# Both output projections of a two-layer encoder by 2x2 blocks with seven block products

## The chip, the core and the metric

The kernel runs on one core of a Trainium2 chip. The metric is the device time of one execution in microseconds. A core has TensorE (PE) for matmuls and transposes, VectorE (DVE), ScalarE (ACT) and GpSimd (POOL) for elementwise work, and SyncE (SP), which here only issues DMAs. Each engine runs its own list of instructions in order; they wait for each other by semaphores.

## What is computed

Two layers over 1024 tokens of width 1024, all in float32. Layer 0 mixes tokens by window attention (16 heads of 64), layer 1 by a gated recurrence in both directions (8 heads of 128); both add four cross-attention heads of 128 into 256 memory tokens. The mixer's output has 1024 + 512 = 1536 columns and goes through one output projection `w_out` (1536 x 1024). Cut to what matters here:

```python
o = jnp.concatenate([o, memory_cross_attn(xq, mem_kv)], axis=-1)   # 1024 x 1536
y = o @ w_out                                                     # the output projection
h = h + rmsnorm(y, norm_g[layer, 1])
v = rmsnorm(h, norm_g[layer, 2])
gate, up = jnp.split(v @ w_in, 2, axis=-1)
f = (jax.nn.gelu(dwconv_centred(gate, conv_w, conv_b)) * up) @ w_out_ffn
h = h + rmsnorm(f, norm_g[layer, 3])
```

## The kernel before

Every float32 product is made of three matmuls: each operand x is split into a high part (a cast by ScalarE) and the rest (a subtraction by VectorE), and hi·hi, lo·hi and hi·lo are summed in PSUM (`mm3`, lines 84 to 86 of the profile; `mmk`, line 529, in the FFN; `split`, lines 89 and 90; `wunit`, lines 79 and 80, for a weight of 128x1024). Inputs come through four stage buffers `st`.

The attention of layer 0 (`window`) goes by four groups of heads: `proj(g)` projects, `attend(g)` does eight blocks of scores, softmax and products with v (tiles `ps`, `pt`, `po`), and the four cross heads are put in as units by the table `XU`. Layer 1 (`hgrn`) goes by eight heads. Both write their outputs, transposed, to DRAM: `oT[l]` has twelve blocks of 128 rows by 1024 tokens, eight of the mixer, four of the cross heads; two blocks are a pair.

The output projection is the class `WOut`. It loads `oT` by token tile (`or`), splits it (`oh`, `ol`), and for each of 8 token tiles, 2 column halves and 12 row blocks issues three matmuls of 128x512 into a PSUM tile `pb`. Its weights are 12 units per layer (`wh`, `xwh`); the first column half stays in `y0` until the second is done. Behind each token tile of the second half come the tile's steps: sum of squares, scale by the norm, add to the residual `x`, store to `h1d`, and `norm_T`, which norms it for the FFN (`nu`, line 115), transposes it by TensorE (`pt`, line 119) and splits it into `uh` and `ul`. Part of the projection begins early: `open` and `early` issue its matmuls among the last attention group and the last head, for the blocks that are there already. A scheduler in the tile framework merges these lists into each engine's order at build time.

The FFN (`ffn`) has both its products by 2x2 blocks with seven block products in place of eight. Its second product has a list `SECOND` of (product, pair) units, `unit` loads a weight block and a block of hidden tokens into one `st` buffer of 128x1024 and splits it, `mms` issues 12 matmuls with it (four token tiles, tiles `X` and `V`). Sums of weight blocks are made in DRAM by accumulating DMAs of GpSimd's queue (`second_sums`), one step at each `sum_steps[l].send(...)`; sums of hidden blocks are made by VectorE and stored in `hid`. The steps behind it, per token tile, are `tail` (lines 790 to 794) and `norm_T`; the first token half's tails come behind pairs 1, 3, 5 and 7 of product 5, the second half's in product 3, for which the last units are held.

## Time and profile before

| | |
|---|---|
| median of 3 runs | 2732.68 us (2732.43 to 2733.03) |
| profiled execution | 2730.88 us, span 2729.1 us |
| mean granted TensorE clock | 0.993 |
| PE busy | 2659.9 us, 97% of the span |
| DVE, ACT, POOL busy | 1825.5, 1390.7, 468.9 us |
| layer 0's projection | about 433.7 (first matmul, among attention) to 597.1 us |
| layer 1's projection | ends at about 2091.5 us |

Times are microseconds from the span's start. In rows of the timeline stand start, duration, engine, line, operation, output<-inputs, form, count, and in brackets the engine's idle time just before and the instruction that ended it. The matmuls overlap in the pipeline, so that the duration of one (0.39 us for 128x512) is longer than the step from one to the next.

### The profile page before, as it was taken

The numbers are of one execution on the slowest core, as the hardware profiler recorded it, in microseconds if no ns is written. First come the engines' busy times: TensorE is split into PE (matmuls) and PEld (weight loads), VectorE is DVE, ScalarE is ACT, GpSimd is POOL, SyncE is SP. The second block draws the span as 40 slices with busy tenths as digits, with TensorE's granted clock in tenths as the row PEclk, the third lists the DMA queues.
The fourth block names the chain that finished last, engine by engine and source line by source line (L and its number), as shares of the span: only waits on it lengthen the run. The fifth ranks groups of instructions, "written<-read, shape, count | busy, mean of one in ns | idle before, by whom it ended". The sixth has DMA issues, their size and how long they took to land.

```text
span 2729.1 us, 37480 instructions
## 1 busy us (share of the span) xinstructions
PE 2659.9 (97%) x13496; PEld 2231.1 (82%) x13496; DVE 1825.5 (67%) x3031; ACT 1390.7 (51%) x2550; POOL 468.9 (17%) x517
## 2 busy tenths in 40 slices
PE   8999998999999999999999999999899999999998
PEld 7888897788888888877888888888788788888886
DVE  6587777578565565477686777868566856566446
ACT  6367666544444444454444545545454444444443
POOL 1231120111111100032232231312121111110013
PEclk9999998999999999999999999999999999999999
DMA  7673213656777757674234541111466587775656
GB/s 278 212 167 95 59 45 100 193 193 150 204 201 194 204 151 241 195 246 140 81 129 114 118 90 55 43 58 34 133 216 171 156 207 202 203 198 158 225 194 228
DMA packets 213580, 428.45 MB, mean 157 GB/s; under 512 B 20369, under 2 KB 77073, under 8 KB 207761
## 3 DMA queue, kind: packets, MB, share of 16 engines
q1 hardware_dynamic: 187264, 333.50, 37.6%
q0 software_dynamic: 23680, 88.09, 15.6%
q10 hardware_dynamic: 2448, 4.46, 0.5%
q8 instruction: 106, 1.74, 0.3%
q14 instruction: 82, 0.66, 0.1%
HBM read 333.17 MB, written 117.96 MB: 165 GB/s over the span
## 4 chain that ended last, share of the span: by engine, by line
PE 86%; DVE 8%; DMA 2%; ACT 2%; issue 2%; POOL 1%; SPq 0%; DVEq 0%; POOLq 0%; ACTq 0%
PE X L529 26%; PE V L529 11%; PE pj L84 7%; PE pj L85 7%; PE pj L86 7%; PE Y L529 5%; PE pb L85 3%; PE pb L84 3%; PE pb L86 3%; PE po L1110 1%; PE pt L341 1%; PE pa L1062 1%; PE pa L1042 1%; PE pu L1086 1%; PE pt L119 1%
## 5 line engine op out<-in xcount | busy, mean ns | idle before, releaser
L90 DVE TENSOR_TENSOR wl<-st,wh 128x1024 fp32r<-128x1024 f32 (+1 forms) x234 | 258.7, 1110 | 338.5 <-ACT wh L89 332.6
L89 ACT CAST wh<-st 128x1024 fp32r<-128x1024 f32 (+1 forms) x234 | 219.1, 938 | 288.1 <-PE X L529 180.2
L84 PE MATMUL pj<-uh,wh 128*128 128x512 f32 x512 | 205.8, 402 | 6.4 <-DVE xl L90 4.6
L529 PE MATMUL X<-wl,wh 128*128 128x512 f32 x528 | 205.1, 390 | 0.1
L529 PE MATMUL X<-wh,wl 128*128 128x512 f32 x528 | 205.0, 390 | 0.0
L86 PE MATMUL pj<-uh,wl 128*128 128x512 f32 x512 | 202.8, 396 | 0.0
L529 PE MATMUL X<-wh 128*128 128x512 f32 x528 | 200.3, 390 | 2.4 <-DVE c L838 1.7
L85 PE MATMUL pj<-ul,wh 128*128 128x512 f32 x512 | 202.2, 395 | 0.1
L84 PE MATMUL pj<-wh,uh 128*128 128x384 f32 (+1 forms) x512 | 191.0, 373 | 0.4 <-DVE v L283 0.4
L85 PE MATMUL pj<-wl,uh 128*128 128x384 f32 (+1 forms) x512 | 187.0, 365 | 0.0
L86 PE MATMUL pj<-wh,ul 128*128 128x384 f32 (+1 forms) x512 | 186.8, 365 | 0.0
L529 PE MATMUL V<-uh,wh 128*128 128x512 f32 x344 | 133.9, 389 | 0.3 <-ACT uh L89 0.3
L529 PE MATMUL V<-ul,wh 128*128 128x512 f32 x344 | 133.9, 389 | 0.0
L529 PE MATMUL V<-uh,wl 128*128 128x512 f32 x344 | 133.9, 389 | 0.0
L80 DVE TENSOR_TENSOR wl<-st,wh 128x1024 fp32r<-128x1024 f32 (+1 forms) x93 | 115.7, 1252 | 25.0 <-ACT wh L79 24.1
L79 ACT CAST wh<-st 128x1024 fp32r<-128x1024 f32 (+1 forms) x103 | 103.9, 1016 | 46.1 <-PE pj L85 27.2
L529 PEld LDWEIGHTS X<-wh 128*128 128x128 f32 x528 | 99.1, 188 | 24.3 <-issue 2.6
L84 PEld LDWEIGHTS pj<-uh,wh 128*128 128x128 f32 x512 | 97.0, 189 | 26.5 <-DVE xl L90 5.5
L1056 POOL TENSOR_TENSOR E<-EP,q 128x256 f32<-128x256 f32 x64 | 54.5, 851 | 371.6 <-DVE EP L1049 292.9
L529 PEld LDWEIGHTS X<-wl,wh 128*128 128x128 f32 x528 | 99.1, 188 | 21.1 <-DVE wl L90 0.5
L529 PEld LDWEIGHTS X<-wh,wl 128*128 128x128 f32 x528 | 99.1, 188 | 20.6
L86 PEld LDWEIGHTS pj<-uh,wl 128*128 128x128 f32 x512 | 96.6, 189 | 19.4
(337 smaller groups left out, 7332.7 us busy)
## 6 DMA issues: line engine op xcount, KB each, us to landing
st<-hid SPq DMA_DIRECT2D x154, 256.0 KB, 3.0
st<-in_ffw_dram SPq DMA_DIRECT2D x106, 256.0 KB, 3.0
w2s<-in_ffw_dram POOLq DMA_DIRECT2D x24, 1024.0 KB, 8.0
st<-in_ffw_dram SPq DMA_DIRECT2D x48, 512.0 KB, 3.6
hid<-tt SPq DMA_DIRECT2D x88, 256.0 KB, 4.5
st<-w2s SPq DMA_DIRECT2D x88, 256.0 KB, 3.1
sx<-in_ffw_dram SPq DMA_DIRECT2D x80, 256.0 KB, 3.9
sy<-in_ffw_dram SPq DMA_DIRECT2D x40, 512.0 KB, 5.7
```

What stands on the lines that cost most here:

```text
L79: act.copy(h[:, :n], raw)
L80: (eng or dve).tensor_tensor(l[:, :n], raw, h[:, :n].bitcast(F32), op=ALU.subtract)
L84: pe.matmul(o, ah, bh, start=first, stop=False)
L85: pe.matmul(o, ah, bl, start=False, stop=False)
L86: pe.matmul(o, al, bh, start=False, stop=last)
L89: act.copy(h, src)
L90: dve.tensor_tensor(l, src, h.bitcast(F32), op=ALU.subtract)
L119: pe.transpose(ps[:, k, :], u[:, (4 * b + k) * P:(4 * b + k + 1) * P], ident)
L341: pe.transpose(tp[:, j, :], sm[:, j, c * P:(c + 1) * P], ident)
L529: pe.matmul(o, x, y, start=new, stop=e, skip_group_check=not first)
L1042: pe.matmul(pa[:, c, :], E2[:, cs], E1[:, cs], start=True, stop=True)
L1056: pool.tensor_tensor(gl, pl_, ql, op=ALU.mult)
```

## The change

The projection is taken out of `WOut` and put on the code of the FFN's second product, which becomes a class `Second` that both use. With the token blocks (rows of the output) split in two halves of 512 tokens, the row blocks in even and odd ones, and the columns of `w_out` in two halves of 512, seven block products replace eight. Per layer there are 7 products x 6 pairs = 42 units, each a weight block and a token block of 128x512, with 12 matmuls a unit, four token tiles of three. The order of products is 1, 2, 6, 7, 4, 5, 3 and that of pairs 0, 1, 2, 4, 5, 3.

`token_sums` makes the sums of token blocks for a pair: it loads two blocks of `oT` into two of the four `st` buffers, does four VectorE operations of 512 columns and stores the buffers to `os`. Sums of weight blocks (`wos`) come from `weight_sums`, 12 more steps ahead of the FFN's 18. The tails come behind pairs 1 to 4 of product 5 and, for the second half, in product 3. `early` issues product 1 of four pairs for three token tiles (layer 0) or two (layer 1) among the last attention group and the last head. Two cross units move from the third attention group to the fourth (`XU`). The first FFN weight is no longer loaded ahead in its own pool.

```diff
-WOUT_POOL = ((0, 1, 2), ())
-XU = [(0, 2), (0, 2), (2, 2), (0, 0)]
+XU = [(0, 2), (0, 2), (2, 0), (2, 0)]
+OLAST, OHOLD = 6, 4
+OPAIRS = (0, 1, 2, 4, 5, 3)
...
-    def second_sums(l):
+    def weight_sums(l):
...
+        for w, o, rs in ((A[f"wout{l}"], wosum[l], (slice(0, 3), slice(3, 6))),
+                         (A["ffw2"][l], w2sum[l], (slice(0, 4), slice(4, 8), slice(8, NP2)))):
+            steps += [(o, r, a, f, n, x, y) for a, f, n, x, y in ((0, 0, 1, w, None), (1, 0, 1, w, None), (2, 2, 2, w, None),
+                                                                  (0, 1, 2, w, True), (2, 0, 1, o, True), (3, 2, 1, o, True)) for r in rs]
...
+    def token_sums(l, p, halves):
+        i, j = (slice(b * 512, (b + 1) * 512) for b in halves)
+        e, c = [stg.tile([P, 1024], F32, tag="st", name="st") for _ in range(2)]
+        nc.sync.dma_start(e, oT[l][2 * p])
+        nc.sync.dma_start(c, oT[l][2 * p + 1])
+        dve.tensor_tensor(c[:, j], c[:, j], e[:, j], op=ALU.subtract)
+        dve.tensor_tensor(e[:, j], e[:, i], e[:, j], op=ALU.subtract)
+        dve.tensor_tensor(e[:, i], c[:, j], e[:, i], op=ALU.add)
+        dve.tensor_tensor(c[:, i], e[:, i], c[:, i], op=ALU.subtract)
+        nc.sync.dma_start(osum[l][p, 0], e)
+        nc.sync.dma_start(osum[l][p, 1], c)
...
         for g in range(3):
             attend(g, cur)
             cur = proj(g + 1)
+            token_sums(0, g, (0, 1))
+            if g == 2:
+                token_sums(0, 4, (0, 1))
+        attend(3, cur)
+        bank = lambda pl, tag, n: pl.tile([P, 512], F32, tag=tag, bufs=n, name=tag)
+        X = lambda t: bank(*((psq, "pj", 2), (psq, "pj", 2), (psq, "ptq", 1), (psp, "po", 1))[t])
+        V = lambda t: bank(psp, *(("ps", 2), ("pt", 2))[t // 2])
+        wo0.early(X, (0, 1, 2), 4)
+        token_sums(0, 5, (0, 1))
+        token_sums(0, 3, (0, 1))
         ea.release()
         ap_.release()
+        wo0.open()
+        return X, V, tags["pt"], (psp, psq)
...
+    class Second:
...
+        def unit(self, k, p):
+            r = stg.tile([P, 2, 512], F32, tag="st", name="st")
+            for i, x in enumerate(self.source(k, p)):
+                nc.sync.dma_start(r[:, i, :], x)
+            held = k == 3 and 0 <= self.pairs.index(p) - (len(self.pairs) - self.last) < self.hold
+            h, l_ = [(self.hold_pool if held else ring).tile([P, 1024], F32R, tag=t, name=t) for t in ("wh", "wl")]
+            r = r.rearrange("p a b -> p (a b)")
+            if k == 6:
+                nsplit(h[:, :512], l_[:, :512], r[:, :512])
+                split(h[:, 512:], l_[:, 512:], r[:, 512:])
+            else:
+                split(h, l_, r)
+            return h, l_
+        def ahead(self):
+            if self.todo and len(self.made) < (self.last if self.todo[0][0] == 3 else 3):
+                self.made.append(self.unit(*self.todo.pop(0)))
+        def mms(self, u, ps, ts_, first):
+            h, l_ = u
+            for t in ts_:
+                m = slice(512 + t * P, 512 + (t + 1) * P)
+                mmk(ps[t], 1, lambda _: (h[:, m], l_[:, m]), lambda _: (h[:, :512], l_[:, :512]), first)
+        def early(self, X, ts_, n):
+            self.X = {t: X(t) for t in ts_}
+            for i in range(n):
+                self.begun.append(self.unit(*self.todo.pop(0)))
+                self.mms(self.begun[-1], self.X, ts_, i == 0)
...
+        def run(self, X, V, free, gy, gx, src, dst, halves):
...
+            tails = (1, 3, 5, 7) if n > 8 else (1, 2, 3, 4)
...
+            for k in self.order:
+                if k == 5:
+                    self.X = {t: X(t) for t in (2, 3, 0, 1)}
+                elif k == 2:
+                    self.V = {t: V(t) for t in range(4)}
+                ps = self.V if k == 2 else self.X
+                hold = []
+                for i, p in enumerate(self.pairs):
+                    if k == 1 and self.begun:
+                        u = self.begun.pop(0)
+                        self.mms(u, ps, rest, i == 0)
+                        self.ahead()
+                        continue
+                    while len(self.made) < 1:
+                        self.ahead()
+                    u = self.made.pop(0)
+                    self.ahead()
+                    if k == 3 and i >= n - self.last:
+                        hold.append(u)
+                    else:
+                        self.mms(u, ps, range(4), k in (1, 5, 2) and i == 0)
+                    if k == 5 and i in tails:
+                        t = tails.index(i)
+                        tail(ia, t, y["c11"][:, t, :], ss["q11"][:, t:t + 1], y["c21"][:, t, :], ss["q21"][:, t:t + 1])
+                for t in range(4):
+                    if k in (1, 6, 7, 4):
+                        act.copy(y[{1: "c11", 6: "c12", 7: "c22", 4: "c21"}[k]][:, t, :], ps[t])
+                    elif k in (2, 5):
+                        q = y[{2: "c11", 5: "c22"}[k]][:, t, :]
+                        dve.tensor_tensor(q, ps[t], q, op=ALU.add)
+                    else:
+                        for u in hold:
+                            self.mms(u, ps, (t,), False)
+                        sb = np_.tile([P, 1], F32, tag="sb", name="sb")
+                        y1 = np_.tile([P, 512], F32, tag="y1", name="y1")
+                        dve.tensor_tensor(y1, ps[t], y["c12"][:, t, :], op=ALU.add)
+                        sumsq(np_, y1, sb)
+                        dve.tensor_tensor(y1, y1, g3[:, D0], op=ALU.mult)
+                        tail(ib, t, y1, sb, y["c22"][:, t, :], ss["q22"][:, t:t + 1])
+                if k == 4:
+                    scaled("c21", "q21", D1)
+                elif k == 5:
+                    scaled("c22", "q22", D1)
+                elif k == 2:
+                    scaled("c11", "q11", D0)
+                    pst[0] = free()
...
+    where = {1: (2, None), 2: (3, None), 4: (1, None), 5: (None, 0), 7: (None, 1), 6: (None, 2), 3: (None, 3)}
+    def block_of(k, p, w, s):
+        a_, d_ = where[k]
+        return w[p, a_] if d_ is None else s[p][d_]
+    def out_proj(l, halves):
+        i, j = (slice(b * 512, (b + 1) * 512) for b in halves)
+        def source(k, p):
+            raw = {1: (0, i), 2: (1, i), 3: (1, j)}
+            made = {6: (0, i), 5: (0, j), 4: (1, i), 7: (1, j)}
+            t = oT[l][2 * p + raw[k][0]][:, raw[k][1]] if k in raw else osum[l][p, made[k][0]][:, made[k][1]]
+            return block_of(k, p, A[f"wout{l}"], wosum[l]), t
+        return Second(l, "wo", OPAIRS, (1, 2, 6, 7, 4, 5, 3), source, OLAST, OHOLD)
...
-                    wo1.early(psj, 2, es)
+                    wo1.early(XB, (0, 1), 4)
             if h == 7:
+                token_sums(1, 5, (1, 0))
...
-                wo1.open(2, 0)
+                wo1.open()
...
+                for p in {1: (0,), 3: (1,), 5: (2, 4)}.get(h, ()):
+                    token_sums(1, p, (1, 0))
+        token_sums(1, 3, (1, 0))
...
-    window()
-    wo0.finish()
-    ffn(0, wo0, h2d, True, (0, 1), (0, 1))
-    hgrn()
-    wo1.finish()
-    ffn(1, wo1, out, False, (1, 0), (1, 0))
+    finish_out(0, wo0, window(), A["x"], (0, 1))
+    ffn(0, h2d, True, (0, 1), (0, 1))
+    finish_out(1, wo1, hgrn(), h2d, (1, 0))```

TensorE's order at the end of layer 0's projection, before (`pb` is the projection, `pt` the transposes of a tile, `X` and `Y` the FFN's first products; the last transposes come 49 rows later):

```order
L85 MATMUL pb_6450<-xwl_5791,oh_6493 128x512
L86 MATMUL pb_6450<-xwh_5790,ol_6494 128x512
L119 MATMUL pt_6436<-ident_74,nu_6429 128x128 x4
L119 MATMUL pt_6443<-ident_74,nu_6429 128x128 x4
L529 MATMUL X_6576<-uh_78,xwh_5796 128x512
L529 MATMUL X_6576<-ul_79,xwh_5796 128x512
...
L529 MATMUL Y_6577<-uh_78,wl_6571 128x512
L529 MATMUL X_6741<-uh_78,wh_6729 128x512
L119 MATMUL pt_6528<-ident_74,nu_6521 128x128 x4
L119 MATMUL pt_6535<-ident_74,nu_6521 128x128 x4
L529 MATMUL X_6741<-ul_79,wh_6729 128x512
```

And now, at the same place (`po` is the last token tile of product 3):

```order
L414 MATMUL po_5978<-wl_6261,wh_6260 128x512
L414 MATMUL po_5978<-wh_6260,wl_6261 128x512
L121 MATMUL pt_6194<-ident_74,nu_6187 128x128 x4
L121 MATMUL pt_6201<-ident_74,nu_6187 128x128 x4
L121 MATMUL pt_6307<-ident_74,nu_6300 128x128 x4
L121 MATMUL pt_6314<-ident_74,nu_6300 128x128 x4
L121 MATMUL pt_6364<-ident_74,nu_6357 128x128 x4
L121 MATMUL pt_6371<-ident_74,nu_6357 128x128 x4
L121 MATMUL pt_6421<-ident_74,nu_6414 128x128 x4
L121 MATMUL pt_6428<-ident_74,nu_6414 128x128 x4
L121 MATMUL pt_6478<-ident_74,nu_6471 128x128 x4
L121 MATMUL pt_6485<-ident_74,nu_6471 128x128 x4
L414 MATMUL X_6531<-uh_78,wh_6519 128x512
```

Five tiles' transposes stand between the projection and the FFN, where two tiles' did, one of them inside the FFN's products. Layer 1 has the same.

SyncE's order where layer 0's projection begins, before (`o` are the attention's last outputs, `or` loads for the projection):

```order
L352 DMA oT0_57<-o_5087 64x2x256 x2
L447 DMA or_5623<-oT0_57 128x2x128
L447 DMA or_5639<-oT0_57 128x6x128
L107 DMA g1_5752<-in_norm_g_dram 128x1024
L107 DMA g2_5754<-in_norm_g_dram 128x1024
```

And now (`st_5356` and `st_5357` are the last token sums, `st_5393` and `st_5403` the last two units of product 1, `st_5413` the first of product 2, in the buffer of `st_5356`):

```order
L370 DMA oT0_57<-o_5145 64x2x256 x2
L154 DMA st_5356<-oT0_57 128x1024
L155 DMA st_5357<-oT0_57 128x1024
L109 DMA g3_5384<-in_norm_g_dram 128x1024
L109 DMA g0_5386<-in_norm_g_dram 128x1024
L435 DMA st_5393<-in_wout0_dram 128x512
L435 DMA st_5393<-oT0_57 128x512
L435 DMA st_5403<-in_wout0_dram 128x512
...
L160 DMA os0_84<-st_5356 128x1024
L161 DMA os0_84<-st_5357 128x1024
L435 DMA st_5413<-in_wout0_dram 128x512
```

A load, four operations and a store stand now between the last output and the loads of product 2.

TensorE's order at the last head of layer 1, before (`po` is the head's output product, `pt` its transposes, 18 rows of `pb` stand between):

```order
L1110 MATMUL po_18099<-S_17366,qin_17364 128x128
L84 MATMUL pb_17859<-xwh_18025,oh_18037 128x512
L85 MATMUL pb_17859<-xwl_18026,oh_18037 128x512
...
L1120 MATMUL pt_18129<-ident_74,on_18124 128x128 x4
L84 MATMUL pb_17902<-xwh_18031,oh_18169 128x512
```

And now (`X` and `pa` are product 1 of the projection):

```order
L1057 MATMUL po_18034<-S_17374,qin_17372 128x128
L1067 MATMUL pt_18064<-ident_74,on_18059 128x128 x4
L414 MATMUL X_17845<-wh_18106 128x512
L414 MATMUL X_17846<-wh_18106 128x512
L414 MATMUL pa_18095<-wh_18106 128x512
```

The head's transposes follow its product at once, and the rest of product 1 follows them.

338 lines of the change are left out of this document (84 added, 254 removed).

## The prediction

> **What bounds the kernel now.** I read the page first. Its rows of busy time and its chain of waits say that TensorE is the kernel:
>
> ```profile
> span 2729.1 us, 37480 instructions
> PE 2659.9 (97%) x13496; PEld 2231.1 (82%) x13496; DVE 1825.5 (67%) x3031; ACT 1390.7 (51%) x2550; POOL 468.9 (17%) x517
> PE 86%; DVE 8%; DMA 2%; ACT 2%; issue 2%; POOL 1%; SPq 0%; DVEq 0%; POOLq 0%; ACTq 0%
> ```
>
> Only 69.2 us of the span are without a matmul. So removed matmuls are worth their full time, but only where TensorE has something else to run meanwhile. The windows show the price of one matmul and the places where TensorE starves already (columns: stretch, length, then busy time and instructions of PE, PEld, DVE, ACT and POOL, granted clock, DMA share, GB/s):
>
> ```profile
> 780.00:840.00 60.00, 60.00 (x266) 49.70 (x265) 33.27 (x36) 26.41 (x34) 8.21 (x10) 1.00 0.79 199
> 400.00:420.00 20.00, 14.27 (x67) 10.80 (x66) 15.86 (x46) 13.43 (x34) 10.66 (x9) 0.87 0.45 145
> 420.00:440.00 20.00, 16.34 (x73) 12.47 (x73) 16.16 (x36) 14.36 (x30) 0.00 (x0) 0.79 0.37 116
> 480.00:500.00 20.00, 17.76 (x89) 13.93 (x88) 11.72 (x21) 12.29 (x27) 0.00 (x0) 1.00 0.25 66
> ```
>
> The first row is the code of the FFN's second product: 60.00/266 gives 0.2256 us per 128x512 matmul; I use 0.2265 (the timeline's rows step by 0.22 to 0.23). The other rows are layer 0's last attention group; after its last projection matmul at 405 us it runs with nothing beside it until the old out-projection begins to fill it:
>
> ```profile
> 405.17 0.38 PE L289 MATMUL ptq<-ident,rq 128*128 128x128 f32 x2
> 433.70 0.50 PE L84 MATMUL pb<-wh,oh 128*128 128x512 f32 x1 [0.68 <-ACT oh L89]
> ```
>
> From 405 to 434 us TensorE idles 5.7 + 3.7 = 9.4 us and its clock falls to 0.8; from 480 to 500 it idles 2.2.
>
> **What it removes.** Per layer the projection has 8 tiles x 2 halves x 12 blocks x 3 = 576 matmuls; seven products of 6 pairs x 4 tiles x 3 are 504. Both layers: 144 x 0.2265 = **-32.6 us**, all on the path. The added splits (42 units of 1024 columns against about 36) and the token sums (24 operations of 0.6 us per layer) lie in stretches like 780 to 840, where VectorE is busy 33 of 60 us; I cost them at nothing there. If that cover went, 12 splits and 24 sums would be 28 us a layer. The weight sums are queued on GpSimd, busy 17%, and paced by steps of the projections and the recurrence far ahead: nothing.
>
> **What it adds at the end of each projection.** Before, the tail of a token tile (add, norm, transposes) comes every 8 us under the next tile's 36 matmuls, and the FFN begins before the last tile is done:
>
> ```profile
> 596.25 1.06 PE L119 MATMUL pt<-ident,nu 128*128 128x128 f32 x8 [0.91 <-DVE nu L115]
> 597.07 0.48 PE L529 MATMUL X<-uh,xwh 128*128 128x512 f32 x1
> 608.47 1.04 PE L119 MATMUL pt<-ident,nu 128*128 128x128 f32 x8
> ```
>
> It costs 0.9 us: the last transposes at 608.47 come inside the FFN's products. Now all eight tails fall into the last two products, and TensorE's order has 40 transposes, each behind VectorE, between the last product and the first FFN matmul. That matmul needs only the first eight of them (the last tile of the first token half) but stands behind all. VectorE's spacing is in these rows:
>
> ```profile
> 1207.38 1.29 DVE L115 SCALAR_TENSOR_TENSOR nu<-x,nrs,g 128x1024 f32<-128x1024 f32 x1 [0.73 <-POOL nrs L96]
> 1208.59 1.22 DVE L90 TENSOR_TENSOR wl<-st,wh 128x1024 fp32r<-128x1024 f32 x1
> 1209.72 0.68 DVE L838 TENSOR_TENSOR c<-X,c 128x512 f32<-128x512 f32 x1
> 1210.32 1.22 DVE L90 TENSOR_TENSOR wl<-st,wh 128x1024 fp32r<-128x1024 f32 x1
> ...
> 1231.75 0.68 DVE L844 TENSOR_TENSOR y<-X,c 128x512 f32<-128x512 f32 x1
> ...
> 1234.84 0.75 DVE L794 SCALAR_TENSOR_TENSOR x<-y,prs,x 128x512 f32<-128x512 f32 x1 [0.66 <-POOL prs L96]
> 1235.51 0.74 DVE L794 SCALAR_TENSOR_TENSOR x<-c,prs,x 128x512 f32<-128x512 f32 x1
> ```
>
> From start to start: a split 1.13, an operation of 512 columns 0.60, a scaled add 0.66, the norm multiply 1.2. From the start of product 5 VectorE has 13 splits (14.7), 16 scaled adds (10.6), 8 norm multiplies (9.6), 16 transposed splits (9.6), 12 adds and multiplies (7.2) and 24 small ones of about 0.1 (2.4): 54 us, and some 4 us of chain waits like the 0.73 and 0.66 above, 58 in all. TensorE has in the same time 12 pairs x 12 x 0.2265 = 32.6 and 64 transposes (8 in 1.04), 8.3: 41 us. It waits 17.3 us. The same tail code already stands behind FFN 0, where the next layer's projections cover it:
>
> ```profile
> 1241.92 0.39 PE L529 MATMUL X<-wh,wl 128*128 128x512 f32 x1
> ...
> 1263.55 0.66 PE L119 MATMUL pt<-ident,nu 128*128 128x128 f32 x4 [0.28 <-DVE ul L90]
> ```
>
> From the last product to the last transposes are 21.9 us, of which the 32 transposes take 4: 18 without cover. Two ways give 17 to 18; I take 17.3. After such a wait the clock is low for a while, as it was here:
>
> ```profile
> 79.00 0.33 PE L289 MATMUL ptq<-ident,rq 128*128 128x128 f32 x1 [2.02 <-POOL rq L279]
> ...
> 80.40 0.52 PE L84 MATMUL pj<-wh,uh 128*128 128x384 f32 x1
> 80.72 0.52 PE L85 MATMUL pj<-wl,uh 128*128 128x384 f32 x1
> ...
> 83.84 0.33 PE L86 MATMUL pj<-wh,ul 128*128 128x384 f32 x1
> ```
>
> Steps of 0.32 instead of 0.17 from 80.4 to 83.6 lose 1.6 us. Per layer 17.3 + 1.6 - 0.9 = 18.0, for both **+36.0**. Bounds: 12 (the first FFN matmul gets in front of some transposes' waits, VectorE without gaps), 23 a layer. The Trainium skill, "TensorE: Matmul & The Clock Gate", section "Part 1: The HAM clock gate", says that an idle window of some 3.4 us halves the clock and that it takes 3.4 us of work to get it back. By that rule a gap costs 1.7 us; but the row above was slow after 2 us idle already, so shorter gaps could cost it too.
>
> **What it adds at the starts.** The last token sums (the pair of heads that is finished last) are a chain through DRAM: store of the head's output, load, four VectorE operations, store. SP issues the loads of the remaining pairs behind that first load, and the first unit of the second product needs a stage buffer that the sums free only when their stores have landed. The DMA rows (count, size, median us from issue to landing):
>
> ```profile
> st<-in_ffw_dram SPq DMA_DIRECT2D x48, 512.0 KB, 3.6
> hid<-tt SPq DMA_DIRECT2D x88, 256.0 KB, 4.5
> st<-hid SPq DMA_DIRECT2D x154, 256.0 KB, 3.0
> oT<-o SPq DMA_DIRECT2D x32, 128.0 KB, 2.4
> oT<-ot SPq DMA_DIRECT2D x16, 256.0 KB, 4.0
> ```
>
> Layer 1, before:
>
> ```profile
> 1946.83 0.89 PE L1110 MATMUL po<-S,qin 128*128 128x128 f32 x4
> 1947.96 0.50 PE L84 MATMUL pb<-xwh,oh 128*128 128x512 f32 x1 [0.24 <-ACT oh L89]
> ...
> 1952.05 0.50 PE L84 MATMUL pb<-xwh,oh 128*128 128x512 f32 x1 [2.42 <-ACT oh L89]
> ...
> 1954.91 0.60 PE L1120 MATMUL pt<-ident,on 128*128 128x128 f32 x4
> 1956.44 0.50 PE L84 MATMUL pb<-xwh,oh 128*128 128x512 f32 x1 [0.93 <-ACT oh L89]
> ```
>
> The last head's transposes come 7.2 us after its last product, and old projection work fills that; 3.6 us are lost. Now nothing stands between. From the end of that product: transposes 7.8, copy 8.4, store 12.4, load 16.0, sums 18.4, store 22.9, load 25.9, cast and split (1.05 + 1.13; the cast's row is below) 28.1. TensorE has 24 matmuls (5.4) and the transposes (0.6): 22.1 idle, **+18.5**. Bounds: +8 if the buffer comes free with the load's consumption, +24 if stores take longer.
>
> ```profile
> L89 ACT CAST wh<-st 128x1024 fp32r<-128x1024 f32 x172 | 180.8, 1053 | 238.5 <-PE X L529 180.2 <-PE V L529 32.1 <-DMA st<-hid 15.4
> ```
>
> Layer 0 has the same chain from its last output: add 1.3, store 3.7, load 7.3, sums 9.7, store 14.2, load 17.2, split 19.4, against 36 matmuls (8.2): 11.2 idle. Ahead of it, only 36 matmuls and two moved cross-attention units fill the last attention group where 150 did, and all of them stand in its first half; the second half (four blocks) is a bare stretch like 405 to 434: 9.4. Less the 2.2 that were idle from 480 to 500: **+18.4**, from +7 to +27. The moved cross units pay for themselves where they left (a matmul there is a matmul here): nothing. The clock is not counted twice, since it was low at these places before. The Trainium skill, "DMA: Bandwidth & Descriptors", section "Anatomy of one DMA — SWDGE (gpsimd) path", puts a transfer at 2.0 us and its bytes at 436 GB/s, which is 3.2 us for 512 KB, and by it layer 1's chain is some 2 us shorter; these rows, 3.6 and 4.5, are of queues in use, and I stay with them.
>
> **Sum.** -32.6 + 36.0 + 18.5 + 18.4 = +40.3, on the profiled execution's 2730.9 us 2771.2. That execution stood 1.8 under the median; against the median I give **2773 us**.
>
> **Rivals.**
> 1. Faster: the waits are filled after all. If the first FFN products, which read the first token half, ran ahead of the second half's transposes, the ends would stay near 0.9 each, and with the starts at their lower bounds (+8, +7) it is -32.6 + 15 = -17.6: about 2715. For it: before, the last transposes did stand inside the FFN's products. Against: the order now has them in front, and at 596.25 the FFN's first matmul waited 0.9 us behind transposes whose tile it does not read. The Trainium skill's TensorE page, in the table of its first part, gives TensorE's queue a partial reorder in which weight loads pass matmuls; by that a matmul does not pass another, as the row shows. Chance 0.08.
> 2. About equal: the ends cost what I say, but the starts nothing, since loads land sooner and cross heads fill: -32.6 + 36 = +3.4, with small remainders 2734 to 2742. Against: the chain through DRAM has four transfers one behind another in any case. Chance 0.13.
> 3. Slower than I say: the whole projection starves, not only its ends. A unit of 512 KB every 12 matmuls (2.7 us) is 190 GB/s, about the 199 of the first window, but a layer's unit goes through 4 stage buffers shared with the sums. If each of 84 units were late by 0.3 us, that is +25: about 2798. For it: pieces of 512 columns from sums that were stored just before. Against: the FFN's second product does this at 60.00 of 60. Chance 0.09.
>
> That the change doesn't remove matmuls can be left out: its order holds 504 per layer.
>
> My forecast keeps 0.70, and its own range, by the bounds above, is 2750 to 2795. With the second rival the range is 2736 to 2797. A measurement of this kernel can tell about 0.2% (5.5 us) from no change, so faster means under 2727: 0.08; between 2727 and 2738, 0.07, the better half of rival 2; the rest, 0.85, slower.
>
> **What would show it.** Per step: 504 matmuls by layer at 0.226; between the last projection matmul and the FFN's first one some 58 - 41 = 17 us without work, ended by VectorE; after the last head of layer 1 a gap of about 22 us ended by loads and splits; in layer 0 two thin stretches of 9 and 11. I am wrong if TensorE's idle time grows by less than 33 us (then it is faster), or if it grows inside the seven products (rival 3).

## The result, and the profile after

The median of four runs is **2806.7 us** (2803.76 to 2810.82), against 2732.6 (2732.43 to 2733.03) of the kernel before: a ratio of 1.0272 (95% interval 1.0254 to 1.0290), 74 us slower. I had said 2773 in 2736 to 2797: the sign was right, the size was not.

From the page of the kernel after, the rows that answer to the first ones of before:

```profile
span 2801.7 us, 37428 instructions
PE 2656.5 (95%) x13352; PEld 2222.9 (79%) x13352; DVE 1883.4 (67%) x3070; ACT 1408.6 (50%) x2538; POOL 505.6 (18%) x554
PE 83%; DVE 6%; DMA 5%; ACT 2%; issue 2%; POOL 1%; SPq 0%; DVEq 0%; POOLq 0%; ACTq 0%
```

There are 144 matmuls fewer, yet TensorE's busy time falls by only 3.4 us of the expected 32.6, and 145.2 us of the span are without a matmul, where it was 69.2. Busy time hides the clock: a matmul at half clock is busy twice as long. So I split each stage into three: idle (length less busy time), clock loss (busy time times one less the granted clock, both summed over windows of 10 us), and the rest, which is work at full clock.

| stage | before | after | idle | clock loss | rest |
|---|---|---|---|---|---|
| start to layer 0's first FFN matmul | 597.1 | 649.7 | 37.1 to 83.7 | 10.4 to 24.4 | 549.5 to 541.6 |
| then to layer 1's last input projection matmul | 1222.8 | 1223.2 | 8.6 to 7.2 | 0.0 to 1.6 | 1214.2 to 1214.3 |
| then to layer 1's first FFN matmul | 259.6 | 281.9 | 11.0 to 44.1 | 1.2 to 8.7 | 247.4 to 229.1 |

Layer 0 loses 52.6 us, layer 1 22.3; what follows is 2.7 shorter. (The table ahead of the prediction ends layer 1's projection at 2091.5, behind the last transposes; by the FFN's first matmul, as in layer 0, it is 2079.5.) Layer 1 came close to the forecast (18.0 + 18.5 - 16.3 = 20.2). Layer 0 did not (18.0 + 18.4 - 16.3 = 20.1).

First the places that I had named. TensorE's rows in the timeline of after, at the start of layer 0's second product, at the end of layer 1's attention, and at the end of layer 0's projection:

```profile
510.10 1.22 PE L414 MATMUL pj<-wh 128*128 128x512 f32 x2 [9.55 <-ACT wh L91]
...
1997.56 1.25 PE L1067 MATMUL pt<-ident,on 128*128 128x128 f32 x4 [5.61 <-DVE on L1063]
2011.35 1.22 PE L414 MATMUL X<-wh 128*128 128x512 f32 x2 [12.54 <-ACT wh L91]
...
634.37 1.97 PE L121 MATMUL pt<-ident,nu 128*128 128x128 f32 x8 [5.96 <-DVE ul L92]
639.69 1.97 PE L121 MATMUL pt<-ident,nu 128*128 128x128 f32 x8 [3.36 <-DVE ul L92]
642.97 1.11 PE L121 MATMUL pt<-ident,nu 128*128 128x128 f32 x4 [1.31 <-DVE ul L92]
644.89 1.12 PE L121 MATMUL pt<-ident,nu 128*128 128x128 f32 x4 [0.81 <-DVE ul L92]
648.10 1.94 PE L121 MATMUL pt<-ident,nu 128*128 128x128 f32 x8 [2.09 <-DVE nu L117]
649.69 0.78 PE L414 MATMUL X<-uh,wh 128*128 128x512 f32 x1
```

The end waits 13.5 us on VectorE in these rows, and 4.46 earlier, at the first tail behind product 5: 18.0 in all, where I had 17.3. Layer 1's start waits 5.61 + 12.54, where I had 22.1. But eight transposes take 1.97 us here and took 1.04 before. The windows of after say why (length, then busy time of PE, PEld, DVE, ACT, POOL, granted clock, DMA share, GB/s):

```profile
634.00:650.00 16.00, 8.07 (x33) 6.50 (x34) 12.24 (x23) 6.29 (x11) 4.01 (x5) 0.50 0.40 145
2139.00:2155.00 16.00, 7.97 (x33) 6.41 (x34) 11.91 (x23) 6.29 (x11) 3.97 (x5) 0.50 0.41 143
510.00:514.00 4.00, 3.90 (x11) 3.15 (x12) 2.45 (x2) 1.08 (x2) 0.00 (x0) 0.62 1.03 420
```

At both ends the clock stands at 0.50 for all of 16 us, and half of the 8 us of work is clock loss. The Trainium skill, "TensorE: Matmul & The Clock Gate", section "Part 1: The HAM clock gate", tells of a half and a full clock, and of some 3.4 us of sustained work to get back to the full one; the trace agrees, since the pieces of work between the waits are 1.1 to 2.0 us, and the clock does not come back in these 16 us. The first 4 us of layer 0's second product stand at 0.62.

Now the place that I had not named: layer 0's third attention group, where the second pair's sums stand. One window of five kernels (before, after, then three experiments told below: without token sums, with late sums, with late sums without their VectorE operations):

```profile
300.00:340.00 40.00, 37.33 (x193) 30.38 (x192) 28.46 (x80) 28.61 (x76) 0.00 (x0) 0.96 0.14 43
```

```profile
300.00:340.00 40.00, 25.00 (x97) 17.83 (x96) 24.65 (x63) 21.28 (x52) 4.08 (x2) 0.74 0.83 228
```

```profile
300.00:340.00 40.00, 39.40 (x237) 35.86 (x236) 32.62 (x88) 28.60 (x74) 5.87 (x9) 1.00 0.80 186
```

```profile
300.00:340.00 40.00, 30.70 (x159) 25.85 (x158) 24.80 (x71) 19.36 (x52) 3.90 (x6) 0.91 0.73 201
```

```profile
300.00:340.00 40.00, 36.64 (x206) 33.13 (x205) 29.90 (x82) 27.49 (x71) 3.92 (x6) 0.96 0.89 230
```

After does 97 matmuls in 40 us, at a clock of 0.74. Without token sums it is 237 at 1.00, with the DMA engines nearly as full (0.80). So a full DMA share alone does not starve TensorE here. What does is in the timeline of after, in the order of the queues:

```profile
276.00 16.77 SPq L370 DMA_DIRECT2D oT<-o  x4
308.56 0.33 SPq L154 DMA_DIRECT2D st<-oT  x1
308.94 0.42 SPq L155 DMA_DIRECT2D st<-oT  x1
309.41 0.43 SPq L80 DMA_DIRECT2D st<-in_wxq_dram  x1
...
324.67 0.69 DVE L156 TENSOR_TENSOR st<-st 128x512 f32<-128x512 f32 x1 [10.76 <-DMA st<-oT]
...
325.98 1.80 ACT L81 CAST wh<-st 128x1024 fp32r<-128x1024 f32 x2 [11.11 <-DMA st<-in_wxq_dram]
...
326.02 1.01 PE L337 MATMUL ps<-kl,qs 128*128 128x384 f32 x2 [8.65 <-DVE kl L92]
```

The sum's load (L154) waits for the store of the group's last head output to land, 9.8 us by the waits of SP's queue, and the next weights (`in_wxq`) stand behind it in that queue: all are issued at 308.56 to 309.41. The loads land only at about 324.7; from 295 to 325 us the DMA engines are full (a share of 0.98 or more), behind six accumulating transfers of GpSimd's weight sums, issued from 289 to 298 (the FFN's, which stand behind the projection's new steps; in the kernel before GpSimd issues none between 241 and 340). The first sum (L156) stands at the head of VectorE's queue until then, the attention's splits (`kl`) and softmax stand behind it, and TensorE waits for `kl`. Without the sums (e2 below) the same weights are issued at 289.67.

### The profile page after: what moved, and what is told of

Read it like the earlier page. It is cut to its first block, busy times and chain, and to the rows that moved or that the text cites. A ratio compares the mean times of both kernels' runs of the same rounds, so it can differ in the third digit from the quotient of the medians.

```text
span 2801.7 us, 37428 instructions
## 1 busy us (share of the span) xinstructions
PE 2656.5 (95%) x13352; PEld 2222.9 (79%) x13352; DVE 1883.4 (67%) x3070; ACT 1408.6 (50%) x2538; POOL 505.6 (18%) x554
## 4 chain that ended last, share of the span: by engine, by line
PE 83%; DVE 6%; DMA 5%; ACT 2%; issue 2%; POOL 1%; SPq 0%; DVEq 0%; POOLq 0%; ACTq 0%
PE X L414 29%; PE V L414 11%; PE pj L86 7%; PE pj L88 7%; PE pj L87 7%; PE Y L414 5%; DMA st<-oT 1%; PE po L1057 1%; PE pa L414 1%; DVE wl L92 1%; PE pa L1009 1%; PE pt L359 1%; PE pj L414 1%; PE pu L1033 1%; PE pa L989 1%
## 5 line engine op out<-in xcount | busy, mean ns | idle before, releaser
L92 DVE TENSOR_TENSOR wl<-st,wh 128x1024 fp32r<-128x1024 f32 (+1 forms) x318 | 358.4, 1135 | 430.6 <-ACT wh L91 424.1
L91 ACT CAST wh<-st 128x1024 fp32r<-128x1024 f32 (+1 forms) x318 | 301.2, 951 | 380.2 <-PE X L414 176.8
L414 PE MATMUL X<-wh 128*128 128x512 f32 x600 | 228.2, 393 | 14.8 <-ACT wh L91 12.9
L414 PE MATMUL X<-wl,wh 128*128 128x512 f32 x600 | 234.3, 392 | 0.2
L414 PE MATMUL X<-wh,wl 128*128 128x512 f32 x600 | 233.8, 391 | 0.0
L86 PE MATMUL pj<-uh,wh 128*128 128x512 f32 x512 | 206.3, 403 | 5.2 <-ACT wh L81 2.7
L508 POOL TENSOR_TENSOR c<-c,g 128x512 f32<-128x512 f32 x48 | 85.2, 1792 | 678.7 <-PE X L414 324.2
L86 PE MATMUL pj<-wh,uh 128*128 128x384 f32 (+1 forms) x512 | 191.0, 373 | 0.0
L414 PEld LDWEIGHTS X<-wh 128*128 128x128 f32 x600 | 113.1, 189 | 39.9 <-ACT wh L91 13.6
L414 PE MATMUL V<-uh,wh 128*128 128x512 f32 x352 | 136.9, 389 | 0.0
L414 PE MATMUL V<-ul,wh 128*128 128x512 f32 x352 | 136.9, 389 | 0.0
L414 PE MATMUL V<-uh,wl 128*128 128x512 f32 x352 | 136.9, 389 | 0.0
L414 PEld LDWEIGHTS X<-wl,wh 128*128 128x128 f32 x600 | 113.2, 189 | 24.6 <-DVE wl L92 1.1
L414 PEld LDWEIGHTS X<-wh,wl 128*128 128x128 f32 x600 | 113.2, 189 | 23.6
L81 ACT CAST wh<-st 128x1024 fp32r<-128x1024 f32 (+1 forms) x88 | 88.6, 1010 | 62.1 <-PE pj L87 25.3
L86 PEld LDWEIGHTS pj<-uh,wh 128*128 128x128 f32 x512 | 97.4, 190 | 25.5 <-ACT wh L81 3.8
L87 PEld LDWEIGHTS pj<-ul,wh 128*128 128x128 f32 x512 | 97.3, 190 | 18.9 <-DVE ul L92 0.4
## 6 DMA issues: line engine op xcount, KB each, us to landing
st<-in_ffw_dram SPq DMA_DIRECT2D x48, 512.0 KB, 3.7
sy<-in_ffw_dram SPq DMA_DIRECT2D x40, 512.0 KB, 5.8
```

The source lines that it names most:

```text
L81: act.copy(h[:, :n], raw)
L86: pe.matmul(o, ah, bh, start=first, stop=False)
L87: pe.matmul(o, ah, bl, start=False, stop=False)
L91: act.copy(h, src)
L92: dve.tensor_tensor(l, src, h.bitcast(F32), op=ALU.subtract)
L414: pe.matmul(o, x, y, start=new, stop=e, skip_group_check=not first)
```

## The experiments

The times are medians; each ratio is against the kernel before, timed beside it, with its 95% interval. The kernel before itself stood at 2729.9 to 2735.4 us, so a difference of two medians that were not taken together can be off by some 5 us. Where a stage is named, its times are those of the profiled executions, which lie up to some 3 us from the medians.

**Which part costs it: weight sums, token sums, or the norm's tails.** Three kernels leave one part out each, a fourth leaves out two.

e1:
```diff
-        for w, o, rs in ((A[f"wout{l}"], wosum[l], ...), (A["ffw2"][l], w2sum[l], ...)):
+        for w, o, rs in ((A["ffw2"][l], w2sum[l], ...),):
```


> Left out: the sums of the projections' weight blocks (24 of the DMA steps of GpSimd's queue over both layers); the units read plain weight blocks in their place, with the same bytes. Theory A (the added weight-sum transfers crowd the DMA engines during layer 0's attention, so that stores and loads of SP's queue land late and TensorE starves between 200 and 330 us): the idle time before layer 0's last attention projection (405 us) falls from 38 us to about 25, as in the kernel before, and the time by some 18 us to 2789. Rival B (it is the place of the token sums in SP's queue alone): no change, 2807 within 4.

2805.0, ratio 1.0274 (1.0258 to 1.0289): in all, the weight sums cost nothing, as rival B said. But at the place above theory A shows: GpSimd issues no DMA there, the DMA engines are idle from 290 to 300 us (a share of 0.01 or less), a sum's load is used 5.9 us after its issue, and TensorE waits 2.25 us and not 8.65. In e1's timeline:

```profile
303.03 0.33 SPq L153 DMA_DIRECT2D st<-oT  x1
...
308.89 0.69 DVE L155 TENSOR_TENSOR st<-st 128x512 f32<-128x512 f32 x1
...
311.90 0.50 PE L86 MATMUL pj<-uh,wh 128*128 128x512 f32 x1 [2.25 <-ACT wh L81]
```

The last input projection matmul of layer 0 comes at 390.5 us for 402.1, and the stretch from there to the FFN is 14.4 us longer (262.0 for 247.6). Why that is so is not shown.

e2:
```diff
 def token_sums(l, p, halves):
+        return
-... else osum[l][p, made[k][0]][:, made[k][1]]
+... else oT[l][2 * p + made[k][0]][:, made[k][1]]
```


> Left out: the sums of token blocks (loads, VectorE operations and stores); the units read plain token blocks in their place. Theory A (weight-sum transfers crowd the DMA engines in layer 0's attention): the stretch between 200 and 330 us stays bad, at least half of its 14 us more idle time remains; only the starts of both projections gain (9.6 us and 12.5 us of wait for a load in the trace), so about 2780. Rival B (the token sums' place in SP's queue): the stretch is as before as well, 18 us more, so about 2763.

2734.6, 1.0017 (1.0007 to 1.0026): the token sums are worth 72 us. Layer 0's first FFN matmul comes at 601.3 for 649.7; of these 48.4 us, 30.6 are idle time and 14.3 clock loss, and 30.8 are lost ahead of the last input projection matmul (371.3 for 402.1).

e4:
```diff
-                if gx is not None:
+                if gx is not None and self.key != "wo":
                     norm_T(np_, pst[0], x, g0, uh, ul, 4 * b + t)
```


> Left out: the norm, transposes and splits for the FFN behind both projections (the FFN reads what stood in its input tiles), so that nothing of VectorE's tails stands between the last product and the FFN's first. My step on the ends, 17 to 18 us idle per layer and in addition a low clock over the last two products and the transposes (about 8 us per layer by the granted clock), plus 64 transposes of 8.3 us: about 2 x 34 less, so 2739. Rival: the FFN's first product waits for its weights or for the residual chain anyway, and the ends keep more than half: above 2770.

2760.9, 1.0110 (1.0093 to 1.0127), 46 us faster than after. The 128 transposes left out are 16.6 of it, and idle time in the two stages from the last input projection to the FFN falls from 89.5 to 58.1. I had expected 68.

e8 is e2 and e4 in one:

> Left out together: the token sums and the norm, transposes and splits for the FFN behind the projections. If the two losses add up (72 us and 46 us when left out singly): 2807 - 118 = 2689. This would also show that the 144 matmuls are worth their 32.6 us: 2730.9 - 32.6 less the 128 transposes (16.6) is 2682, to which thin attention in layer 0 adds some. Rival (the removed matmuls had filled waits that remain): above 2705.

2692.9, 0.9850 (0.9834 to 0.9867): the two costs add up, but for 4 us. Up to layer 1's first FFN matmul the rest, work at full clock, is 1961.4 us against 2011.1 before: 49.7 less, where 32.6 of matmuls and 16.6 of transposes make 49.2. The matmuls give what they should.

**What about the sums: their place, their bytes, their operations.** e3 issues layer 0's sums one group later, and in both layers the last two pairs' sums behind the first units of product 2:

```diff
-            token_sums(0, g, (0, 1))
-            if g == 2:
-                token_sums(0, 4, (0, 1))
+            if g > 0:
+                token_sums(0, g - 1, (0, 1))
...
-        token_sums(0, 5, (0, 1))
-        token_sums(0, 3, (0, 1))
+        token_sums(0, 2, (0, 1))
+        token_sums(0, 4, (0, 1))
+        wo0.sums = [lambda p=p: token_sums(0, p, (0, 1)) for p in (5, 3)]
...
+                    if k == 2 and i in (0, 2) and self.sums:
+                        self.sums.pop(0)()
```


> The same work in another place: each group's token sums in layer 0 come one group later, and the last two pairs' sums in both layers behind the first units of product 2, which read plain blocks and do not need them. If the order of SP's queue is what makes the waits (B, and my step on the starts): the starts gain some 20 us and the stretch from 200 to 330 us some 12, so about 2775. If the DMA engines are short there (A): the stretch from 200 to 330 stays, and only the starts gain, 2787. Rival C (the sums only move their wait into products 1 and 2): 2800.

2771.7, 1.0157 (1.0142 to 1.0173): 35 us back. Layer 1's start falls from 12.54 to this, in the timeline of e3:

```profile
2004.49 0.74 PE L414 MATMUL X<-wh 128*128 128x512 f32 x2 [3.77 <-ACT wh L91]
```

e5 moves only the last two pairs' sums, in both layers:

> Only the sums of the last two pairs of each layer go behind the first units of product 2; the four other pairs' sums stay in their place. My step on the starts (18.5 in layer 1 and 9 to 11 in layer 0, because the last pair's sums stand ahead of loads that do not need them): some 19 us less in layer 1 and 8 in layer 0, so about 2780, and the idle time before layer 0's last attention projection stays at 38 us. Rival (the starts are bound by the store and load of the last heads themselves): under 8 us less, 2800.

2784.3, 1.0190 (1.0175 to 1.0206). Layer 1 gets 14.7 us back, layer 0 only 3.3: its 38 us of idle time ahead of the last input projection matmul stay.

e6 leaves out the sums' four VectorE operations (L156 to L159) and keeps their loads and stores; e7 gives them to GpSimd (`dve.` becomes `pool.`):

> Left out: only the 48 VectorE operations of the token sums; their loads and stores stay where they are. If VectorE is what stalls in layer 0's attention (theory D: a sum's first operation stands at the head of VectorE's queue until its load has landed, 10.8 us in the trace, and the splits that TensorE needs stand behind it): the extra 14 us of idle time before 405 us go, and with some clock about 18 to 20 us, so 2787. If SyncE's queue is (theory S: projection weights are issued behind the sums' loads, which wait for the attention's stores): no more than 5 us, so above 2802.

> The sums' 48 operations run on GpSimd in place of VectorE, at the same place. Theory D (VectorE's queue): VectorE is free of the stall, so near the kernel without these operations; but GpSimd's other work, the last step of rotation (rq) and the norm powers, then stands behind the same load, so between 2787 and 2800. Theory S (SyncE's queue): 2807 or more, since an operation of 512 columns takes GpSimd 1.3 us or more and the stage buffers are held longer.

2811.2, 1.0286 (1.0271 to 1.0302), and 2820.3, 1.0319 (1.0304 to 1.0335). Both lie where theory S put them, and the operations seem to cost nothing. I took this for the end of the theory of VectorE's queue. It was too early: the next weights stand behind the sums' loads in SP's queue (`in_wxq` is issued at 312.99) and land as late as these, so that TensorE now waits for them, as the timeline of e6 shows:

```profile
328.57 1.04 ACT L81 CAST wh<-st 128x1024 fp32r<-128x1024 f32 x1 [11.36 <-DMA st<-in_wxq_dram]
...
329.67 0.80 PE L86 MATMUL pj<-uh,wh 128*128 128x512 f32 x1 [10.43 <-ACT wh L81]
```

e13 keeps the order and cuts each transfer to 64 of 1024 columns; e14 keeps the bytes and takes the wait for the store away by loading rows of the input `x`:

```diff
-        nc.sync.dma_start(e, oT[l][2 * p])
+        nc.sync.dma_start(e[:, :64], oT[l][2 * p][:, 960:])     # e13
+        nc.sync.dma_start(e, A["x"][p * P:(p + 1) * P, :])      # e14
...
```


> The token sums in their place in the changed kernel, with every load, operation, store, buffer and wait, but each transfer moves 64 of the 1024 columns (the last ones, which are stored last), and the units read plain token blocks. If it is waits and order (W: SyncE stands at a sum's load until the attention's last store has landed, and projection weights stand behind it): most of the 72 us stays, above 2780. If it is bytes (Y: 2 MB of sums per pair crowd the DMA engines, so that all transfers land late): nearly as without token sums, 2734 to 2750.

> The token sums with all bytes, operations, stores and buffers, but they load other data (rows of the input x, there from the start), so that no load of a sum waits for a store of the attention; the units read plain token blocks. W (waits and order): most of the 72 us goes, 2735 to 2760. Y (bytes): most of it stays, above 2780.

2788.4, 1.0207 (1.0192 to 1.0223), and 2783.6, 1.0188 (1.0171 to 1.0205). Taking away the bytes gave 18 of the 72, taking away the wait for the store 23: e13 came out where W had put it, e14 where Y had, so neither theory is enough alone. By the stages, e13's gain is not at the place that it tested: layer 0 gains 1.8 us, layer 1's stage 12.7. e14 gains 18.9 in layer 0 and 13.1 in layer 1's stage, and loses 10.4 in the stage between. In e13's timeline the gap is still there:

```profile
309.91 0.33 SPq L154 DMA_DIRECT2D st<-oT  x1
...
323.89 0.19 DVE L158 TENSOR_TENSOR st<-st 128x32 f32<-128x32 f32 x1 [12.34 <-DMA st<-oT]
...
325.54 0.79 PE L365 MATMUL po<-pl,v 128*128 128x512 f32 x1 [12.48 <-DVE pl L92]
```

A load of a sixteenth of the bytes took 14 us to land, where the whole one took 16. And e14 takes away only the wait for the store: its loads at this place, issued at 298.64 and 302.09, are landed at 317.79, with the DMA engines full (0.96 or more from 290 to 320), and VectorE waits 10.89 us for them.

**Buffers and queues.** On e3, e9 gives layer 0's sums two small buffers of their own (pieces of half the columns, so twice the transfers), and e10 also issues them from GpSimd's queue:

```diff
...
+            for q in range(2):
+                e, c = [tsp[0].tile([P, 2, 256], F32, tag="ts", name="ts") for _ in range(2)]
...
+                nc.sync.dma_start(e, part(oT[l][2 * p]))        # e9
+                pool.dma_start(e, part(oT[l][2 * p]))           # e10, in its place
...
```


> On the kernel with late sums (2771.7): layer 0's token sums get two buffers of their own (128x512, so each pair in two pieces) and no longer take two of the four stage buffers. If it is the stage buffers (theory S1: projection weights wait for a buffer that a sum holds from its load to the landing of its stores): the idle time before layer 0's last attention projection falls from 30 to about 23 us, and the time by 10 to 15 us, to 2759. If it is the order of SyncE's queue (S2: weights stand behind a sum's load that waits for the attention's stores): 2772 within 4.

> As the kernel with own buffers, and layer 0's sums are loaded and stored by GpSimd's queue in place of SyncE's. S2 (SyncE's order): SyncE is free of them, so layer 0 comes near the kernel without token sums (33 us from it with late sums): at least 15 us less than with own buffers alone, about 2748. Rival (GpSimd's queue, where the weight sums run and the rotation's last step is issued, stalls in the same way): no gain or a loss, 2765 or more.

2781.4, 1.0183 (1.0168 to 1.0198): buffers of their own do not help; the kernel is 10 us slower, with twice the transfers, and what each of the two does is not told apart. 2768.5, 1.0136 (1.0121 to 1.0151): the other queue gives 13 back. SP issues `in_wxq` at 292.07 us in e10, where it was 304.40 in e9, so a good part of e9 was standing in SP's line. But e10 is no better than e3 by more than 3: GpSimd now stands 9.4 us ahead of the sum's load, and TensorE waits 4.54 us for the rotation's last step (`rq`) behind it, as the rival said.

**With the late sums, what is left of the 37 us.** On e3: e16 leaves out the projection's weight sums (as e1), e17 the sums' VectorE operations (as e6), e18 cuts the transfers (as e13).

> The kernel with late sums (2771.7) without the projection weight sums: their DRAM traffic is gone and the products read plain weight blocks, so the result is another. Leaving the sums out altogether gave 2734.6, so 37 us are to be had. If the weight sums' transfers keep the late sums' transfers slow (theory G), 2745 to 2757. If what is left is VectorE's operations (theory V) or the sums' own bytes (theory Y), 2768 to 2775.

> The kernel with late sums without the sums' four VectorE operations: loads and stores stay, so the result is another. Theory V, by which 24 operations of 0.6 us in layer 0's attention (14 us) delay the splits and the softmax behind them in VectorE's queue now that no operation there waits for a slow load: 2745 to 2760. Theories G and Y: 2768 to 2775.

> The kernel with late sums, each of their transfers cut to 64 of 1024 columns; the products read plain blocks, so the result is another. The order and the number of transfers stay, bytes and nearly all VectorE time of the sums go. Theory Y (bytes) or V (operations): 2735 to 2750, and with the run before it tells which of the two. Theory G, or transfers counted by number and not by size: 2765 to 2772.

2768.5, 1.0127 (1.0112 to 1.0142); 2751.9, 1.0066 (1.0049 to 1.0083); 2757.5, 1.0090 (1.0074 to 1.0106). e18 falls between the ranges of its theories. The operations that were worth nothing in e6 are worth 20 us here (22.3 in layer 0 by the profiled executions, and nothing in layer 1; by the ratios, 25). Their own work in layer 0 is some 14 us at 0.6 each, beside other work, so that some of it is waiting. Rows of e3's timeline:

```profile
311.96 0.33 SPq L154 DMA_DIRECT2D st<-oT  x1
...
316.66 0.69 DVE L156 TENSOR_TENSOR st<-st 128x512 f32<-128x512 f32 x1 [9.48 <-DMA st<-oT]
317.27 0.61 DVE L339 CUSTOM_DVE_ANT_0 sm<-ps,wmask,sk 128x384 f32<-128x384 f32 x1
...
317.94 0.69 PE L336 MATMUL ps<-kh,qs 128*128 128x384 f32 x1 [6.04 <-DVE mx L339]
```

The softmax's maximum (L339) stands behind a sum that waits 9.48 us, first for its load to be issued (at 311.96, when the store before it has landed) and then for the load, and TensorE waits for the maximum. Here the sums hold up no weights that TensorE needs next, so that VectorE's wait is the one that ends last. But this place is the smaller part: e17 gains 4.9 us up to the last input projection matmul and 17.4 behind it, where eight of the operations stand between 429 and 439 us and eight between 499 and 519. What delays TensorE there was not followed step by step.

**Toward a version that wins.** On e3, e11 loads and splits four of product 3's six units early, in products 7 and 4, and e12 has product 5's gain multiplies on VectorE, not GpSimd:

```diff
+                    if self.key == "wo" and k in (7, 4) and i in (2, 4):        # e11
+                        self.held.append(self.unit(3, self.pairs[len(self.held)]))
-                pool.tensor_tensor(y[q][:, t, :], ...)                          # e12
+                (dve if q == "c22" and self.key == "wo" else pool).tensor_tensor(y[q][:, t, :], ...)
```


> On the kernel with late sums (2771.7): four of the six units of product 3 are loaded and split during products 7 and 4, in the held buffers that stand empty then. It takes 4 x 1.13 = 4.5 us of VectorE's work out of the last two products. My step on the ends (VectorE's 54 us of work against TensorE's 41 set them): 4.5 us less per layer, 2763. Rival (the tails' chain over ScalarE, GpSimd and VectorE sets the ends, not VectorE's load): less than 2 us per layer, above 2768.

> On the kernel with late sums (2771.7): the four multiplications by the norm's gain that follow product 5 run on VectorE (0.6 us each) in place of GpSimd, where two took 5.6 us and the norm power of the next tile stood behind them. If VectorE's plain load is all that counts: 2.4 us more per layer, 2776. If GpSimd's work beside it is what stretches the end (VectorE's norm multiply took 2.3 us in place of 1.3 while it ran, and VectorE waited 1.7 us for the power): 2 to 4 us less per layer, 2766.

2764.4, 1.0125 (1.0109 to 1.0140), and 2766.6, 1.0132 (1.0115 to 1.0149): 7 and 5 us. e12 came about as expected, 2.3 us in layer 0 and 1.9 in layer 1's stage. e11 met its total and not its split: 4.5 a layer were expected, and it is 6.6 in layer 0 and 0.2 in layer 1's stage, so that its account of the ends is not shown. e15 keeps the old projection in layer 0 and takes seven products in layer 1 alone, with late sums and both of these:

> Layer 0 keeps the projection of the kernel before; layer 1 has the seven products with the last sums late, four units of product 3 early and the gain of product 5 on VectorE. Layer 1's stretch from its last projection matmul to the FFN's first was 259.6 us before, and with late sums 263.1, with the gain on VectorE 261.2, with early units 262.9: so about 261, and the time within 2 us of before, 2730 to 2733. Rival (the two edits add up better without layer 0's losses): 2725.

2733.55, 1.0006 (0.9997 to 1.0015): equal to before. Layer 1's stage is 263.7 us, where it was 259.6, and no version here with the full computation beats the kernel before.

## Why the prediction was right and wrong

- **Matmuls, -32.6.** Right, by e8. In after itself, in layer 1 the rest falls by 18.3 (16.3 predicted), in layer 0 by only 7.9; where the other 8 went is not settled.
- **The ends, 17.3 us of waits a layer.** Right: 18.0 and, added up in the same way, 19.6. e4 shows the place: without the tails the idle time of the two stages falls by 31.4.
- **Layer 1's start, 22.1 idle.** Right in mechanism, a little long: 5.61 + 12.54 + 1.77 = 19.9. e3 and e5 cut it to 7.0 and 6.8 by moving the last sums.
- **Layer 0's start.** The wait of 11.2 is 9.55 + 1.39. The chain was right. The thin second half of the last attention group, 9.4, is 8.5 (460 to 500 us of after).
- **The clock after a wait, 1.6 us at each end and nothing at the starts.** Mis-sized: clock loss grew by 14.0 in layer 0 and 7.5 in layer 1; the last 16 us of each end alone lose 4.0, and the first 4 us of layer 0's start 1.5. I had taken one gap and its recovery; a row of short gaps holds the clock at 0.50 through the 16 us shown. And "the clock is not counted twice, since it was low at these places before" was wrong, since the new waits made more such places.
- **"The added splits ... and the token sums ... I cost them at nothing there."** This is the step that failed, for the token sums. I priced them as VectorE work in stretches where VectorE has room, and only the last pair's as a chain. The first ones stand in layer 0's attention, ahead of the next group's weights in SP's queue and ahead of the softmax and the splits in VectorE's, with a load that can't start before a store has landed and then takes 16 us. The prediction named what is behind them in neither queue. By the profiled executions of after and e2 they cost 48.4 us in layer 0 and 16.9 in layer 1 (18.5 with the stage ahead of it); I had 11.2 and 18.5. The 37 that layer 0 has too much are the miss: 2773 and 37 make 2810. The bound given for a lost cover (28 us a layer, from their durations) was of the wrong kind: an operation in line costs its wait.
- **"The weight sums ...: nothing."** Right in the total (e1), and not in the mechanism: their transfers fill the DMA engines when the token sums' loads are issued.
- **The range.** The bounds of the terms add up to 2739 and 2797 against the median, where 2750 and 2795 were given by them; 2806.7 lies above either. Rival 3 had the whole projection starving, by 0.3 us a unit; in after no wait of 1 us stands in TensorE's rows between 511 us and the tails at 606. The size it gave was nearer than mine, its mechanism was not the one.

Shown: 35 of the 72 us go with the sums' place (e3), 20 more with their VectorE operations once the place is another (e17). The last 17 stay open. The weight sums are 3 of them by the medians and 8 by the ratios (e16): without them layer 0 gains 11.8 us, and the stages behind it lose 5.7 again, for a reason not shown. The sums' bytes give at most e18's 14, which can't be told from shorter waits in VectorE's queue, since a smaller transfer also shortens these.

Why the loads at 308 us take 16 us is shown in part. They are slow where GpSimd's accumulating transfers (six, issued from 289 to 298 in after) have filled the DMA engines, whatever their own size (e13) and without the store ahead of them (e14), and quick in e1, where these transfers are not there, and in e3, where the load is issued 17 us behind the last of them. But full engines are not enough: without token sums (e2) they are as full, at 0.98 or more from 285 to 315 us, and TensorE is busy all through, since its weights had been issued by 289.67 and nothing of VectorE stood behind a sum's load. In after the two come together: a late load, and queues that stand still for it.

## What to carry to other kernels

Price a step that goes through DRAM by where it stands in each in-order queue, the issuing one and the consuming one: what is behind it there waits out its store and its load, and the work itself is the small part. Two queues that wait for the same load hide each other: take away one and TensorE waits as long for the other (e6). Read by stages where an experiment gains its time: e13 tested a place in layer 0 and gained in layer 1, and e1 lost behind a place what it had gained there. Where short waits of TensorE follow one another, count the work between them at half clock.

## What was not expected of the hardware

- A load's time depended on the moment more than on its size. After's median is in its list of DMA issues:

```profile
st<-oT SPq DMA_DIRECT2D x24, 512.0 KB, 4.2
```

  Yet the pair issued at 308.56 had landed only at 324.67, and in e13 one of a sixteenth of the bytes took 14 us there. In e1 the load issued at 303.03 was used at 308.89, in e3 the one issued at 311.96 at 316.66. The windows in which they were under way, of after, e1 and e3, differ in the share of the DMA engines that is busy (1.03, 0.44, 0.52):

```profile
310.00:315.00 5.00, 2.42 (x6) 1.62 (x7) 2.56 (x7) 4.87 (x14) 0.00 (x0) 0.66 1.03 253
300.00:305.00 5.00, 5.00 (x34) 4.66 (x33) 1.92 (x7) 0.89 (x3) 1.17 (x2) 1.00 0.44 124
310.00:315.00 5.00, 1.90 (x12) 1.40 (x10) 0.00 (x0) 0.00 (x0) 0.00 (x0) 1.00 0.52 194
```

- The Trainium skill, "DMA: Bandwidth & Descriptors", section "Issuing engines are not separate DMA queues", says that issuing from several engines only saves the time of issuing, usually small. Here e10 gained 13 us over e9 by it: what it saves is also the waiting in line behind a DMA whose semaphore has not come.
- VectorE's norm multiply took twice its time beside GpSimd's gain multiplies. Rows of after's timeline:

```profile
616.65 3.53 POOL L508 TENSOR_TENSOR c<-c,g 128x512 f32<-128x512 f32 x2
...
616.71 2.31 DVE L117 SCALAR_TENSOR_TENSOR nu<-x,nrs,g 128x1024 f32<-128x1024 f32 x1 [1.70 <-POOL nrs L98]
620.72 1.28 DVE L117 SCALAR_TENSOR_TENSOR nu<-x,nrs,g 128x1024 f32<-128x1024 f32 x1 [0.44 <-POOL nrs L98]
```

  It took 2.31 us beside the pair at 616.65 and 1.28 after it. With product 5's multiplies on VectorE (e12) none of the 32 norm multiplies takes more than 1.29, and the kernel is 5 us faster.
